# Gate tiles shared between VectorE and GpSimd, and the softmax totals brought to their rows by fewer transfers

## The chip, the cores and the metric

The kernel runs on one core of one Trainium2 chip. The metric is the device time of one execution in microseconds; the time shown for a kernel is the median of its runs. A profile of a single execution lists, per engine, every instruction with its start and its duration: PE (TensorE) multiplies matrices, DVE (VectorE) and POOL (GpSimd) do elementwise arithmetic, ACT (ScalarE) does functions, copies and roundings, and SP (SyncE) only issues DMA transfers, in order, from one queue. Every engine takes its instructions in the order in which they were laid down; an instruction that has to wait holds up all that stand behind it.

## The reference

One layer of a decoder trunk over x of 512 tokens by 2048 channels, all in float32:

```python
mod = silu(c) @ w_ada + b_ada                      # 2048 -> 6144
shift, scale, gate = split(mod, 3)
h = rms_norm(x, norm_g) * (1 + scale) + shift
z = h @ w_in                                       # columns: u_a v_a g_a q_b k_b v_b g_b f_b
y_a = u_a' * (tril(w_s) @ LayerNorm(v_a') + b_s) * silu(g_a)     # 8 groups, chunks of 128 tokens
y_b = softmax(q k^T / 8 + F[t] - F[s], causal) @ v * silu(g_b)   # 16 heads of 64, F = cumsum(log sigmoid f)
out = rms_norm(x + gate * (concat(y_a, y_b) @ w_out), final_g)
```

Two pieces matter here. The vector **gate**, the last third of `mod`, is a product of a vector of 2048 with a matrix of 2048 by 2048 and is needed only when the output projection is done. The **softmax** is normalised ahead: the logarithm of each row's total is subtracted inside the exponent, so the totals have to get into an operand of the score matmul.

## The kernel before, in words

**Products.** Every float32 operand of a large matmul is taken apart into a rounded upper part (hi) and the remainder (lo), and each product is three matmuls: hi by hi, hi by lo, lo by hi (L147 to L149 with the weights as the stationary operand, L156 to L158 with the tokens). `w_tile` loads one weight tile of 512 KB into a buffer named `raw` (L125), ScalarE rounds it to `whi` (L131), VectorE subtracts to get `wlo` (L132). There are four `raw` buffers and two each of `whi` and `wlo`. A weight tile of the second half feeds 24 matmuls of 128x512.

**Order.** The instruction order of each engine is not the order of the text. A planner with a timeline model of its own lays the instructions out; `tc.high_priority(offset=150)` in `w_tile` lets a weight tile's load and split be drawn ahead of other work, and `tc.issue_after(ins)` pins an instruction behind `ins` in the queue of the engine that both use. After each weight tile, `tick()` runs one entry of `slots` (attention or mixer steps) and one entry of `fillers` (side work).

**The gate.** 32 of the fillers are `gate_step(g, i)`, for g of 0 to 3 (512 columns each) and i of 0 to 7. Each loads a gate tile, two blocks of 128x512 (L601), into the same four `raw` buffers that the weight tiles use; GpSimd multiplies each block by its column of silu(c) (L606, L608) and adds it to `gate[:, g, :]` (L609). `gate_sum(g)` then adds over the partitions with a matmul by ones (L668) and adds the bias (L669). After the gates, `sum_part` fills the ticks with sums of output weights on GpSimd (L654).

**The softmax totals.** For each of four groups u of four heads, `score_head` computes the row maxima `nm` and the totals `rs` (both 128 partitions by 16: four heads by four blocks of tokens), and `lse()` takes the logarithm (L502), subtracts (L503), transposes the 128x16 block on TensorE (L505), takes the result apart into hi and lo (`lt`, L66 on ScalarE and L67 on VectorE) and writes each head's hi row and lo row into two rows of the second query operand `QS[i][1]`, with one DMA from SP for each row: 8 transfers of 2 KB (L512). `probs(i)` multiplies that operand in L529. `lt` in the trace is the source of these transfers and `q` their destination.

**Around it.** In the order of the trace: norm and conditioning, the first big column groups (st), value products of group A (va), then the attention part (q, k, gb, vb groups, four times), and the output projection (wo). The lines at issue lie in the attention part.

Of the kernel before, what the change touches and what calls it, by code (L numbers as in the profile page):

```python
# [8 lines left out]
F32 = mybir.dt.float32  # L9
F32R = mybir.dt.float32r  # L10
BF16 = mybir.dt.bfloat16
AF = mybir.ActivationFunctionType
ALU = mybir.AluOpType
AX = mybir.AxisListType

P = 128
# [11 lines left out]
def trunk_kernel(  # L28
# [17 lines left out]
    nc = tc.nc  # L46
# [12 lines left out]
    def bank(tag, name):  # L59
        if tag == "x":  # L60
            tag = "bbbc"[turn[0] % 4]
            turn[0] += 1
        return ps.tile([P, 512], F32, tag=tag, name=name, bufs={"mm": 4, "b": 3, "c": 1}[tag])

    def split(hi, lo, src, eng=None):
        a = nc.scalar.activation(hi, src, AF.Copy)  # L66
        return a, (eng or nc.vector).tensor_tensor(lo, src, hi.bitcast(F32), ALU.subtract)  # L67


    ident = const.tile([P, P], F32, name="ident")  # L70
# [45 lines left out]
    WPRI = 150  # L116
    EPRI = 150

    def w_tile(segs, k0, nk, src=win_r, name="", pri=WPRI, loeng=None):
        n = sum(w for _, w in segs)  # L120
        with tc.high_priority(offset=pri):
            raw = wp.tile([P, nk, n], F32, tag="raw", name=f"raw_{name}", bufs=4)
            o = 0
            for c0, w in segs:
                newest_w[0] = (load if pri == 0 else nc.sync.dma_start)(  # L125
                    raw[:, :, o : o + w], src[:, k0 : k0 + nk, c0 : c0 + w]
                )
                o += w
            hi = wp.tile([P, nk, n], F32R, tag="whi", name=f"whi_{name}")
            lo = wp.tile([P, nk, n], F32R, tag="wlo", name=f"wlo_{name}")  # L130
            nc.scalar.activation(hi, raw, AF.Copy)  # L131
            (loeng or nc.vector).tensor_tensor(lo, raw, hi.bitcast(F32), ALU.subtract)  # L132
        return hi, lo
# [72 lines left out]
    sc = const.tile([P, KB], F32, name="sc")  # L206
# [10 lines left out]
    gate = gp_.tile([P, 4, 512], F32, name="gate")  # L217
# [135 lines left out]
    def new_y(b):  # L353
        y[b] = act.tile([P, S], F32, tag="ya" if b < 8 else "yb", bufs=8, name=f"y{b}")
# [7 lines left out]
    for q, (k0, nk) in enumerate(CH):  # L362
# [10 lines left out]
        for si, sid in enumerate(order):  # L373
# [9 lines left out]
            for kk in range(k0, k0 + nk, st_k):  # L383
                for gi, (segs, bl) in enumerate(grp):
                    hi, lo = w_tile(
                        segs, kk, st_k, name=f"st{q}_{sid}_{gi}_{kk}", pri=0,
# [29 lines left out]
    pb = ctx.enter_context(tc.tile_pool(name="pb", bufs=1))  # L416
    QS, KS = [], []
# [18 lines left out]
    def halves(e):  # L436
        return (slice(0, 64), slice(64, 128)) if e == 0 else (slice(64, 128), slice(0, 64))
# [35 lines left out]
    def attention_slots(u):  # L473
        nms, rss, lts = {}, {}, {}
        ptt = {}

        def score_head(i):
            if i == 0:
                nms[0] = pb.tile([P, 16], F32, name=f"nm{u}", tag="nm", bufs=1)
                rss[0] = pb.tile([P, 16], F32, name=f"rs{u}", tag="rs", bufs=1)  # L480
            nm, rs = nms[0], rss[0]
            q1, q2 = QS[i]
            k1, k2 = KS[i]
            for t in range(NT):
                n = (t + 1) * P
                tsl = slice(t * P, n)
                cx = slice(4 * i + t, 4 * i + t + 1)
                s_ = bank("x", f"s{u}_{i}_{t}")
                nc.tensor.matmul(s_[:, 0:n], q1[:, tsl], k1[:, 0:n], start=True, stop=False)
                nc.tensor.matmul(s_[:, 0:n], q2[:, tsl], k2[:, 0:n], start=False, stop=True)  # L490
                nc.vector.tensor_tensor_reduce(
                    out=s_[:, 0:n], in0=s_[:, 0:n], in1=cmask[:, S - n : S], scale=1.0,
                    scalar=3.0e38, op0=ALU.add, op1=ALU.min, accum_out=nm[:, cx],
                )
                nc.scalar.activation(
                    s_[:, 0:n], s_[:, 0:n], AF.Exp, bias=nm[:, cx], scale=-1.0,
                    accum_out=rs[:, cx],
                )

        def lse():  # L500
            nm, rs = nms[0], rss[0]
            nc.scalar.activation(rs, rs, AF.Ln)  # L502
            nc.vector.tensor_tensor(nm, nm, rs, ALU.subtract)  # L503
            lp = bank("x", f"lse{u}")
            nc.tensor.transpose(lp[0:16, 0:P], nm, ident)  # L505
            lt = pb.tile([16, 2, P], F32R, name=f"lt{u}", tag="lt", bufs=1)
            split(lt[:, 0, :], lt[:, 1, :], lp[0:16, 0:P])
            for i in range(4):
                _, o = halves(i % 2)
                s2 = QS[i][1]  # L510
                for r_ in range(2):
                    nc.sync.dma_start(  # L512
                        s2[o.start + r_ : o.start + r_ + 1, :].bitcast(F32),
                        lt[4 * i : 4 * i + 4, r_, :].bitcast(F32),
                    )

        def probs(i):
            h = 4 * u + i
            q1, q2 = QS[i]
            k1, k2 = KS[i]  # L520
            pth = pb.tile([P, 1280], F32R, name=f"pth{h}", tag="pth")
            ptl = pb.tile([P, 1280], F32R, name=f"ptl{h}", tag="ptl")
            ptt[i] = (pth, ptl)
            for j in range(NT):
                n = S - j * P
                ssl = slice(j * P, (j + 1) * P)
                t_ = bank("x", f"t{h}_{j}")
                nc.tensor.matmul(t_[:, 0:n], k1[:, ssl], q1[:, j * P : S], start=True, stop=False)
                nc.tensor.matmul(t_[:, 0:n], k2[:, ssl], q2[:, j * P : S], start=False, stop=True)  # L529
                nc.vector.tensor_tensor(t_[:, 0:P], t_[:, 0:P], cmaskT, ALU.add)  # L530
                pr = pb.tile([P, S], F32, name=f"p{h}_{j}", tag="p", bufs=2)
                nc.scalar.activation(pr[:, 0:n], t_[:, 0:n], AF.Exp, scale=-1.0)
                osl = slice(OFF[j], OFF[j] + n)
                split(pth[:, osl], ptl[:, osl], pr[:, 0:n])

        def values(i):
            h = 4 * u + i
            b = 2 * u + i // 2
            e = i % 2
            pth, ptl = ptt[i]  # L540
            op = bank("x", f"o{h}")
            for buf in (pth, ptl):
                for j in range(NT):
                    nc.tensor.matmul(
                        op[:, j * P : S], vs_[0][:, j, i, :], buf[:, OFF[j] : OFF[j] + S - j * P],
                        start=(buf is pth and j == 0), stop=(buf is ptl and j == NT - 1),
                    )
            a, o = halves(e)
            if e == 0:
                new_y(8 + b)  # L550
            tm = pb.tile([P, S], F32, name=f"tm{h}", tag="th", bufs=2)
            nc.scalar.activation(tm[a], op[o], AF.Copy, scale=0.5)
            late = b not in sgb
            nc.vector.scalar_tensor_tensor(
                y[8 + b][a] if late else tm[a], op[a], 0.5, tm[a], ALU.mult, ALU.add
            )
            if not late:
                nc.vector.tensor_tensor(y[8 + b][a], tm[a], sgb[b][a], ALU.mult)

        c_ = lambda f, *a: (lambda: f(*a))  # L560
        return [
            [c_(score_head, 0), c_(score_head, 1)],
            [c_(score_head, 2), c_(score_head, 3)],
            [c_(lse)],
            [c_(probs, 0)],
            [c_(values, 0), c_(probs, 1)],
            [c_(values, 1), c_(probs, 2)],
            [c_(values, 2), c_(probs, 3)],
            [c_(values, 3)],
        ]  # L570
# [28 lines left out]
    def gate_step(g, i):  # L599
        ga = wp.tile([P, 2, 512], F32, tag="raw", name=f"gate{g}_{i}", bufs=4)  # L600
        nc.sync.dma_start(ga, ada_r[:, 2 * i : 2 * i + 2, 2, g * 512 : (g + 1) * 512])  # L601
        for j in range(2):
            kk = 2 * i + j
            a = gate[:, g, :]
            if kk == 0:
                nc.gpsimd.tensor_scalar(a, ga[:, j], sc[:, 0:1], None, ALU.mult)  # L606
            else:
                nc.gpsimd.tensor_scalar(ga[:, j], ga[:, j], sc[:, kk : kk + 1], None, ALU.mult)  # L608
                nc.gpsimd.tensor_tensor(a, a, ga[:, j], ALU.add)  # L609


    dram = ctx.enter_context(tc.tile_pool(name="dram", bufs=1, space=bass.MemoryType.DRAM))
# [203 lines left out]
    for g in range(4):  # L816
        for i in range(8):
            gates.append(lambda g=g, i=i: gate_step(g, i))
            if g and i == 2:
                gates.append(lambda g=g: gate_sum(g - 1))  # L820
# [73 lines left out]
    r = [[None] * 4 for _ in range(NT)]  # L894
# [259 lines left out]
```

## Time and profile before

| what | value |
|---|---|
| median of 3 runs | 905.56 us (905.46 to 912.02) |
| the profiled execution: its time | 903.07 us |
| the profiled execution: its span, first to last instruction | 901.3 us |
| mean granted TensorE clock | 0.988 |
| busy: PE, DVE, ACT, POOL | 878.5, 596.3, 444.6, 438.1 us |

The span is what the rows of the trace add up to; the time of the execution holds 1.8 us around it. Rows of instruction groups give line, engine, operation, output<-inputs by the program's names, shapes, count | busy us, mean ns of one | idle us of the engine just before them and what ended it. Rows of a timeline give start, duration, engine, line and operation. Rows of waits give engine, line and the releaser: total us, times, longest us.

### The profile page before, as it was taken

The numbers are of one execution on the slowest core, as the hardware profiler recorded it, in microseconds if no ns is written. First come the engines' busy times: TensorE is split into PE (matmuls) and PEld (weight loads), VectorE is DVE, ScalarE is ACT, GpSimd is POOL, SyncE is SP. The second block draws the span as 40 slices with busy tenths as digits, with TensorE's granted clock in tenths as the row PEclk, the third lists the DMA queues.
The fourth block names the chain that finished last, engine by engine and source line by source line (L and its number), as shares of the span: only waits on it lengthen the run. The fifth ranks groups of instructions, "written<-read, shape, count | busy, mean of one in ns | idle before, by whom it ended". The sixth has DMA issues, their size and how long they took to land.

```text
span 901.3 us, 12686 instructions
## 1 busy us (share of the span) xinstructions
PE 878.5 (97%) x4408; PEld 744.5 (83%) x4408; DVE 596.3 (66%) x982; ACT 444.6 (49%) x775; POOL 438.1 (49%) x338
## 2 busy tenths in 40 slices
PE   6999999999999999999999999999999999999995
PEld 4988888887888997778789888998898888888884
DVE  4768888374436866455786563456764679997687
ACT  5653332442213224465666554557465657554454
POOL 2355555425676359988998879444751000000001
PEclk7899999999999999999999999999999999999998
DMA  9999996438996164554554545677576246577575
GB/s 339 352 352 356 354 318 212 121 108 292 312 317 201 40 186 124 161 161 133 174 165 140 166 130 187 199 234 221 186 249 188 71 126 209 182 252 248 177 238 203
DMA packets 139712, 188.91 MB, mean 210 GB/s; under 512 B 9968, under 2 KB 103360, under 8 KB 139136
## 3 DMA queue, kind: packets, MB, share of 16 engines
q1 hardware_dynamic: 139216, 187.53, 65.0%
q8 instruction: 35, 0.57, 0.3%
q10 hardware_dynamic: 432, 0.57, 0.2%
q14 instruction: 29, 0.24, 0.1%
HBM read 166.90 MB, written 20.97 MB: 208 GB/s over the span
## 4 chain that ended last, share of the span: by engine, by line
PE 88%; DVE 4%; DMA 3%; issue 2%; ACT 2%; POOL 0%; SPq 0%; POOLq 0%; ACTq 0%; DVEq 0%
PE s L149 6%; PE s L147 6%; PE s L148 6%; PE vb L156 3%; PE vb L157 3%; PE vb L158 3%; PE va L158 3%; PE va L156 3%; PE va L157 3%; PE q L147 3%; PE q L149 3%; PE q L148 3%; PE gb L149 3%; PE k L149 3%; PE gb L148 3%; PE gb L147 3%
## 5 line engine op out<-in xcount | busy, mean ns | idle before, releaser
L608 POOL TENSOR_SCALAR gate<-gate,sc 128x512 f32<-128x512 f32 x60 | 106.4, 1783 | 22.6 <-DMA gate<-in_w_ada_dram 13.6
L132 POOL TENSOR_TENSOR wlo_st<-raw_st,whi_st 128x1024 fp32r<-128x1024 f32 (+3 forms) x36 | 68.4, 1905 | 51.3 <-ACT whi_st L131 48.0
L609 POOL TENSOR_TENSOR gate<-gate,gate 128x512 f32<-128x512 f32 x60 | 91.7, 1530 | 1.8
L148 PE MATMUL s<-hl,whi_st 128*128 128x512 f32 x224 | 86.8, 390 | 0.0
L147 PE MATMUL s<-hh,whi_st 128*128 128x512 f32 x224 | 86.7, 392 | 0.0
L654 POOL TENSOR_TENSOR ts<-ts 128x256 f32<-128x256 f32 x64 | 57.1, 898 | 58.2 <-DMA ts<-in_w_out_dram 55.3
L66 ACT ACTIVATE whi_p<-p 128x1024 fp32r<-128x1024 f32 x52 | 55.2, 1061 | 55.1 <-PE woZ L938 20.1
L67 DVE TENSOR_TENSOR wlo_p<-p,whi_p 128x1024 fp32r<-128x1024 f32 x52 | 63.4, 1221 | 20.2 <-ACT whi_p L66 20.1
L246 DVE SCALAR_TENSOR_TENSOR acc<-ada,sc,acc 128x512 f32<-128x512 f32 x98 | 73.9, 754 | 3.4 <-DMA ada<-in_w_ada_dram 0.5
L149 PE MATMUL s<-hh,wlo_st 128*128 128x512 f32 x224 | 76.2, 392 | 0.0
L157 PE MATMUL vb<-whi_vb,hl 128*128 128x256 f32 (+1 forms) x256 | 72.2, 285 | 0.0
L156 PE MATMUL vb<-whi_vb,hh 128*128 128x256 f32 (+1 forms) x256 | 72.0, 285 | 0.0
L158 PE MATMUL vb<-wlo_vb,hh 128*128 128x256 f32 (+1 forms) x256 | 71.3, 288 | 0.0
L981 POOL TENSOR_TENSOR sfin<-sfin,nhalf 128x1 f32<-128x1 f32 x2 | 1.5, 748 | 137.7 <-DVE sfin L1073 137.7
L131 ACT ACTIVATE whi_st<-raw_st 128x1024 fp32r<-128x1024 f32 (+3 forms) x36 | 31.3, 871 | 65.1 <-PE s L148 38.8
L147 PE MATMUL q<-hh,whi_q 128*128 128x512 f32 x128 | 50.6, 395 | 1.3 <-ACT whi_q L131 1.3
L132 DVE TENSOR_TENSOR wlo_va<-raw_va,whi_va 128x1024 fp32r<-128x1024 f32 x16 | 26.0, 1626 | 38.0 <-ACT whi_va L131 33.9
L147 PE MATMUL k<-hh,whi_k 128*128 128x512 f32 x128 | 50.2, 392 | 0.7 <-ACT whi_k L131 0.7
L147 PE MATMUL gb<-hh,whi_gb 128*128 128x512 f32 x128 | 50.4, 394 | 0.3 <-ACT whi_gb L131 0.3
L156 PE MATMUL va<-whi_va,hh 128*128 128x512 f32 x128 | 50.3, 393 | 0.0
L148 PE MATMUL q<-hl,whi_q 128*128 128x512 f32 x128 | 50.2, 392 | 0.0
L148 PE MATMUL gb<-hl,whi_gb 128*128 128x512 f32 x128 | 50.2, 392 | 0.0
(308 smaller groups left out, 2541.9 us busy)
## 6 DMA issues: line engine op xcount, KB each, us to landing
ada<-in_w_ada_dram SPq DMA_DIRECT2D x128, 256.0 KB
gate<-in_w_ada_dram SPq DMA_DIRECT2D x32, 512.0 KB
p<-ts SPq DMA_DIRECT2D x32, 512.0 KB
p<-in_w_out_dram SPq DMA_DIRECT2D x24, 512.0 KB
raw_va<-in_w_in_dram SPq DMA_DIRECT2D x16, 512.0 KB
raw_q<-in_w_in_dram SPq DMA_DIRECT2D x16, 512.0 KB
raw_k<-in_w_in_dram SPq DMA_DIRECT2D x16, 512.0 KB
raw_gb<-in_w_in_dram SPq DMA_DIRECT2D x16, 512.0 KB
```

The source lines that it names most:

```text
L67: return a, (eng or nc.vector).tensor_tensor(lo, src, hi.bitcast(F32), ALU.subtract)
L132: (loeng or nc.vector).tensor_tensor(lo, raw, hi.bitcast(F32), ALU.subtract)
L147: nc.tensor.matmul(pt, hi[:, j, cs], hh[k], start=(k == first), stop=False)
L148: nc.tensor.matmul(pt, hi[:, j, cs], hl[k], start=False, stop=False)
L149: nc.tensor.matmul(pt, lo[:, j, cs], hh[k], start=False, stop=(k == last))
L156: nc.tensor.matmul(o, ah[k][:, tsl], hi[:, j, :], start=(k == first), stop=False)
L157: nc.tensor.matmul(o, al[k][:, tsl], hi[:, j, :], start=False, stop=False)
L158: nc.tensor.matmul(o, ah[k][:, tsl], lo[:, j, :], start=False, stop=(k == last))
L246: nc.vector.scalar_tensor_tensor(sb if kk == KB - 1 else a, ga[:, j], col, a, ALU.mult, ALU.add)
L608: nc.gpsimd.tensor_scalar(ga[:, j], ga[:, j], sc[:, kk : kk + 1], None, ALU.mult)
L609: nc.gpsimd.tensor_tensor(a, a, ga[:, j], ALU.add)
L654: nc.gpsimd.tensor_tensor(dst, l, r, ALU.subtract)
```

## The change

First, in `gate_step`, every second tile (i even) is multiplied and summed on VectorE: one tensor_scalar and one scalar_tensor_tensor make `p`, the weighted sum of the two blocks, in place; GpSimd adds `p` to the accumulator in one instruction. For i = 0, VectorE writes the accumulator itself and GpSimd does nothing. Tiles with i odd are done on GpSimd as before.

Second, in `lse`, the split into hi and lo comes before the transpose: ScalarE rounds the 128x16 block, VectorE subtracts, into one tile `n2` ordered by head, part and token block; one transpose of 128x32 and one ScalarE copy make `lt` of 32 rows, in which a head's hi and lo rows stand together, so one transfer of 8 pieces brings both: four transfers instead of eight.

Third, in `w_tile`, a list `pins`: of the weight tiles that follow an `lse` in the text, the fifth is issued behind that `lse`'s last row transfer.

```diff
+    pins = []
+
     def w_tile(segs, k0, nk, src=win_r, name="", pri=WPRI, loeng=None):
         n = sum(w for _, w in segs)
-        with tc.high_priority(offset=pri):
+        es = ExitStack()
+        for p in list(pins):
+            p[0] -= 1
+            if p[0] < 0:
+                es.enter_context(tc.issue_after(p[1].ins))
+                pins.remove(p)
+        with es, tc.high_priority(offset=pri):
             raw = wp.tile([P, nk, n], F32, tag="raw", name=f"raw_{name}", bufs=4)
...
             lp = bank("x", f"lse{u}")
-            nc.tensor.transpose(lp[0:16, 0:P], nm, ident)
-            lt = pb.tile([16, 2, P], F32R, name=f"lt{u}", tag="lt", bufs=1)
-            split(lt[:, 0, :], lt[:, 1, :], lp[0:16, 0:P])
+            n2 = pb.tile([P, 4, 2, 4], F32R, name=f"n2_{u}", tag="n2", bufs=1)
+            split(n2[:, :, 0, :], n2[:, :, 1, :], nm.rearrange("p (i t) -> p i t", t=4))
+            nc.tensor.transpose(lp[0:32, 0:P], n2.rearrange("p i r t -> p (i r t)").bitcast(F32), ident)
+            lt = pb.tile([32, P], F32R, name=f"lt{u}", tag="lt", bufs=1)
+            nc.scalar.activation(lt, lp[0:32, 0:P], AF.Copy)
             for i in range(4):
                 _, o = halves(i % 2)
-                s2 = QS[i][1]
-                for r_ in range(2):
-                    nc.sync.dma_start(
-                        s2[o.start + r_ : o.start + r_ + 1, :].bitcast(F32),
-                        lt[4 * i : 4 * i + 4, r_, :].bitcast(F32),
-                    )
+                rows_in = nc.sync.dma_start(
+                    QS[i][1][o.start : o.start + 2, :].bitcast(F32),
+                    lt[8 * i : 8 * i + 8, :].bitcast(F32),
+                )
+            pins.append([4, rows_in])
...
         nc.sync.dma_start(ga, ada_r[:, 2 * i : 2 * i + 2, 2, g * 512 : (g + 1) * 512])
+        a = gate[:, g, :]
+        if i % 2 == 0:
+
+            p = ga[:, 0] if i else a
+            nc.vector.tensor_scalar(p, ga[:, 0], sc[:, 2 * i : 2 * i + 1], None, ALU.mult)
+            nc.vector.scalar_tensor_tensor(
+                p, ga[:, 1], sc[:, 2 * i + 1 : 2 * i + 2], p, ALU.mult, ALU.add
+            )
+            if i:
+                nc.gpsimd.tensor_tensor(a, a, p, ALU.add)
+            return
         for j in range(2):
             kk = 2 * i + j
-            a = gate[:, g, :]
-            if kk == 0:
-                nc.gpsimd.tensor_scalar(a, ga[:, j], sc[:, 0:1], None, ALU.mult)
-            else:
-                nc.gpsimd.tensor_scalar(ga[:, j], ga[:, j], sc[:, kk : kk + 1], None, ALU.mult)
-                nc.gpsimd.tensor_tensor(a, a, ga[:, j], ALU.add)
+            nc.gpsimd.tensor_scalar(ga[:, j], ga[:, j], sc[:, kk : kk + 1], None, ALU.mult)
+            nc.gpsimd.tensor_tensor(a, a, ga[:, j], ALU.add)
```

## The prediction, made before the changed kernel ran

> **What bounds the kernel now.** I read the busy table first, then the stretch in which both edits lie (windows), then what TensorE waited for in it.
>
> ```profile
> span 901.3 us, 12686 instructions
> PE 878.5 (97%) x4408; PEld 744.5 (83%) x4408; DVE 596.3 (66%) x982; ACT 444.6 (49%) x775; POOL 438.1 (49%) x338
> ```
>
> ```profile
> 330.00:430.00 100.00, 97.21 (x451) 78.95 (x451) 55.17 (x85) 49.59 (x95) 87.62 (x54) 1.00 0.49 155
> 430.00:564.00 134.00, 133.21 (x718) 115.38 (x719) 84.69 (x150) 76.85 (x158) 119.51 (x79) 1.00 0.51 157
> 564.00:745.00 181.00, 180.11 (x1029) 158.70 (x1028) 111.19 (x221) 107.67 (x226) 65.11 (x75) 1.00 0.60 186
> ```
>
> ```profile
> PE q L147 <- ACT whi_q L131: 1.3, 1, 1.3
> PE t L529 <- DMA q<-lt: 0.9, 1, 0.9
> PE o L544 <- DVE ptl L67: 0.8, 1, 0.8
> PE k L147 <- ACT whi_k L131: 0.7, 1, 0.7
> PE gb L147 <- ACT whi_gb L131: 0.3, 1, 0.3
> PE k L149 <- DVE wlo_k L132: 0.3, 1, 0.3
> ```
>
> TensorE is busy 97% of the span, and the edits take no matmul from it: the transpose is still one instruction, wider by 16 columns. So they can win only TensorE's idle time where gates and totals are made. The windows (length; busy PE, PEld, DVE, ACT, POOL; clock) give it: 100 - 97.21 = 2.79 us, 134 - 133.21 = 0.79, 181 - 180.11 = 0.89, together **4.47 us**; the six longest waits add up to 4.3 of it. The granted clock is 1.00 throughout, so the throttle plays no part. The other idle time, in the first 50 us and in the last 50, is out of reach.
>
> GpSimd is nearly full there (87.62 of 100 and 119.51 of 134). Yet it is not TensorE that waits for it, but SP:
>
> ```profile
> SPq L125 <- POOL gate L609: 51.3, 18, 9.6
> SPq L601 <- POOL gate L609: 23.4, 7, 8.1
> ```
>
> ```profile
> 345.52 0.37 SPq L125 DMA_DIRECT2D raw_k<-in_w_in_dram  x1
> 354.10 0.37 SPq L601 DMA_DIRECT2D gate<-in_w_ada_dram  x1
> 354.56 0.42 SPq L125 DMA_DIRECT2D raw_k<-in_w_in_dram  x1
> ```
>
> ```profile
> 393.32 1.68 DVE L132 TENSOR_TENSOR wlo_gb<-raw_gb,whi_gb 128x1024 fp32r<-128x1024 f32 x1 [2.16 <-ACT whi_gb L131]
> 395.05 0.50 PE L149 MATMUL gb<-hh,wlo_gb 128*128 128x512 f32 x1
> ```
>
> ```profile
> 545.67 1.23 DVE L132 TENSOR_TENSOR wlo_k<-raw_k,whi_k 128x1024 fp32r<-128x1024 f32 x1 [4.42 <-ACT whi_k L131]
> 551.25 0.39 PE L149 MATMUL k<-hh,wlo_k 128*128 128x512 f32 x1
> ```
>
> A gate tile sits in a `raw` buffer until GpSimd is through, and SP's queue stood 51.3 + 23.4 = 74.7 us behind such buffers. At 345.52 to 354.10 a gate load holds up the weight load behind it. What reaches TensorE depends on the lead of the weights. At 393 us the remainder tile is ready at 393.32 + 1.68 = 395.00 and used at 395.05: no lead. At 545 us it is ready at 546.90 and used at 551.25: 4.35 us. So in 330 to 430 weights come just in time, and 2.79 of the 4.47 us are lost there; later the lead hides most of GpSimd's lateness.
>
> **The change part by part.** The gate arithmetic:
>
> ```profile
> L608 POOL TENSOR_SCALAR gate<-gate,sc 128x512 f32<-128x512 f32 x60 | 106.4, 1783 | 22.6 <-DMA gate<-in_w_ada_dram 13.6 <-issue 6.4 <-DVE vs L67 2.4
> L609 POOL TENSOR_TENSOR gate<-gate,gate 128x512 f32<-128x512 f32 x60 | 91.7, 1530 | 1.8
> L606 POOL TENSOR_SCALAR gate<-gate,sc 128x512 f32<-128x512 f32 x4 | 8.3, 2076 | 2.2 <-DMA gate<-in_w_ada_dram 2.1
> L768 DVE TENSOR_SCALAR va<-va,mv,rsv 128x512 f32<-128x512 f32 x8 | 4.7, 616 | 0.4 <-POOL rsv L91 0.4
> L986 DVE TENSOR_SCALAR c<-c,sfin 128x512 f32<-128x512 f32 x4 | 1.8, 480 | 0.0
> L246 DVE SCALAR_TENSOR_TENSOR accs<-ada,sc,accs 128x512 f32<-128x512 f32 x10 | 7.5, 751 | 0.7 <-DMA ada<-in_w_ada_dram 0.5
> ```
>
> *Off GpSimd:* 16 of the 32 tiles lose both multiplications (4 of L606, 28 of L608) and, per g, four of 15 additions (one for i = 0; one each for i = 2, 4, 6): 4 x 2.076 + 28 x 1.783 + 16 x 1.530 = 82.7 us of 206.4. All of it lies beside TensorE and is worth nothing itself; it is worth the earlier buffers.
>
> *On VectorE:* 16 tensor_scalar, between 0.480 and 0.616 us, and 16 scalar_tensor_tensor at 0.751: 19.7 to 21.9 us, 1.37 us a pair at most. VectorE is busy 55.17 + 84.69 of 234 us there and would come to about 160. The cover is the weights' lead: with 4.35 us a pair costs nothing; with 0.05 us it costs TensorE what it delays, unless the weights come sooner.
>
> *A wait moves with it.* The first VectorE instruction of a pair waits for the gate tile's transfer; behind it stand `wlo`, the softmax rows and the evacuations, and TensorE waits for those. GpSimd's waits of this kind show the size (13.6 us in 12 of 32 tiles; half the tiles would give about 7 us):
>
> ```profile
> POOL gate L608 <- DMA gate<-in_w_ada_dram: 13.6, 12, 2.9
> ```
>
> *The totals:*
>
> ```profile
> 418.34 6.34 SPq L512 DMA_DIRECT2D q<-lt  x8
> 424.80 0.37 SPq L125 DMA_DIRECT2D raw_q<-in_w_in_dram  x1
> ...
> 495.98 5.09 SPq L512 DMA_DIRECT2D q<-lt  x8
> 604.01 5.22 SPq L512 DMA_DIRECT2D q<-lt  x8
> 686.73 5.26 SPq L512 DMA_DIRECT2D q<-lt  x8
> ```
>
> ```profile
> 424.80 3.93 DMA raw_q<-in_w_in_dram
> 428.75 1.06 ACT whi_q L131
> 429.86 0.50 PE q L147
> ```
>
> ```profile
> L502 ACT ACTIVATE rs<-rs 128x16 f32<-128x16 f32 x4 | 0.9, 216 | 0.0
> ```
>
> Eight issues hold SP for 5.09 us at least, 0.64 each; four at that price 2.5 us. The transfer of eight pieces instead of four isn't in the trace; I bound it by 0.37 (the weight load's row) and twice 0.64, and take 0.64, the nearest kind. SP gets back 21.9 - 10.2 = 11.7 us. The chain of waits shows where that counts: the weight load at 424.80 stood behind the eight rows, landed 3.93 us later, and TensorE began its tile at 429.86 after the 1.3 us wait of the list above. Four rows end some 3 us earlier: that 1.3 us goes. The 0.9 us (L529 waiting for the rows of the last group) goes too: its rows left SP from 686.73 on, head 0 needs one transfer instead of two, and the pin keeps a weight load of that time behind the rows. Against it: the chain gains a hop, a ScalarE rounding before the transpose (0.22 us by L502's row, 1.06 more, as at 428.75, if a `whi` split stands in front). I cost this at nothing, covered by the halved queue; uncovered, 0.2 to 1.3 us in each of four groups.
>
> *What is left of the waits.* 0.7 and 0.3 (the k group at 363 us, behind the late load at 354.56): I count 0.7 won. 0.8 (`ptl`): half. The 0.3 of gb: 0.2. Sum of gains: 1.3 + 0.9 + 0.7 + 0.4 + 0.2 = **3.5 us**, bounds 0 and 4.5. What is added: GpSimd's 87.62 us in 330 to 430 are some 14 gate tiles (206.4 / 32 = 6.45 us each), so seven become pairs; most meet a longer lead than now because SP is freed; I charge **1.0 us**, bounds 0 and the second rival's 9. Net -2.5: an execution of 903.07 would become 900.6. It lies 2.5 us under the median of the runs, 905.56, and I forecast against the latter: **903.0 us**.
>
> The two elementwise engines slow each other here:
>
> ```profile
> 445.77 4.25 DVE L132 TENSOR_TENSOR wlo_k<-raw_k,whi_k 128x1024 fp32r<-128x1024 f32 x1 [1.03 <-ACT whi_k L131]
> 445.75 2.53 POOL L609 TENSOR_TENSOR gate<-gate,gate 128x512 f32<-128x512 f32 x2
> 448.26 1.56 POOL L608 TENSOR_SCALAR gate<-gate,sc 128x512 f32<-128x512 f32 x1
> ```
>
> This subtraction takes 1.23 us at 545.67 and 4.25 us beside three gate instructions of GpSimd: 3.0 us lost in one instruction. [...] In the sum I let it cancel: 82.7 us less GpSimd also block `wlo` less.
>
> **The rivals.**
>
> *All of the waits go.* GpSimd's gate work is then 40% lighter, the ring of `raw` buffers never holds SP, and the pairs are hidden: -4.5 us, 901.0. For it: the 74.7 us of SP; against it: the 0.8 us has another cause.
>
> *VectorE takes the place of GpSimd: slower.* Place: 330 to 430 us. It decides from the point where what stands ahead of a `wlo` exceeds the weights' lead there (0.05 us at 393). Price: a pair of 1.37 us, plus a mean wait for its tile of 13.6 / 12 = 1.1, less about 1 us of lead, 1.5 us on each of seven tiles, is 10; less the waits won, +7 to +10 us: 913 to 916. A single block of 3.0 us per pair would give more. For it: VectorE waits in order, GpSimd's lateness hurt only through the ring. Against it: VectorE is idle 45% of that stretch.
>
> *The change doesn't do what it says.* The ring is released no earlier, because an even tile now waits for VectorE's queue and then for GpSimd's, and the rows leave no earlier, because the extra hop eats the shorter queue. Then all the waits stay, if in another place: 905.5, within 1.5.
>
> **How the numbers follow.** Forecast 0.50; all waits gone or a little better 0.12; no change 0.22; VectorE 0.16, of which half stays under 1% because the lead has grown. One per cent is 9 us, about what a measurement of this kernel can tell from no change. Faster by over 1% would need twice the idle time found, by another layout of the planner: 0.04 of the second case. So faster 0.04, slower 0.08, within 0.88. Range: below, 901.0 less the 2.5 us by which executions of one kernel differ, 898.5; above, into the VectorE case, 909.5.
>
> **What would show it.** Right: gate instructions of GpSimd at about 124 us, four row transfers of 2 to 3 us per group, SP's wait for L609 well under 74.7 us, TensorE's idle time in these stretches near 2 us. Wrong: VectorE idle ahead of the pairs on gate transfers over 7 us, `wlo` ready later than TensorE wants it in 330 to 430, TensorE waiting on L529 for the rows in more than one group, or a changed tail after 850 us.

## The result: slower by 0.6%, and where the profile after shows it

The changed kernel takes 911.26 us (median of 22 runs, 909.13 to 917.14), the kernel before 904.88 us beside it; the ratio is 1.0062, with an interval of 1.0046 to 1.0079. The forecast was 903.0, in a range of 898.5 to 909.5, so sign and range were both missed. Executions of one kernel differ by the clock granted in the first 50 us of the span (0.69 in some of the profiled ones, 0.83 to 0.90 in the others), so what is compared below are the measured ratios with their intervals, which are not the quotients of the medians.

The busy table and the three stretches of the changed kernel, columns as before:

```profile
span 908.1 us, 12618 instructions
PE 881.1 (97%) x4408; PEld 745.5 (82%) x4408; DVE 614.2 (68%) x1014; ACT 445.3 (49%) x779; POOL 357.4 (39%) x290
...
330.00:430.00 100.00, 96.26 (x446) 78.30 (x445) 60.68 (x96) 48.64 (x94) 52.14 (x34) 1.00 0.53 161
430.00:564.00 134.00, 130.64 (x693) 111.39 (x692) 92.55 (x167) 76.02 (x159) 71.91 (x51) 0.99 0.49 150
564.00:745.00 181.00, 179.63 (x1028) 158.52 (x1027) 108.47 (x212) 105.14 (x222) 66.37 (x74) 1.00 0.57 180
```

GpSimd is 80.7 us lighter (82.7 were worked out). TensorE's idle time went up: 3.74 us in the first stretch (2.79 before), 3.36 in the second (0.79), 1.37 in the third (0.89), together 8.47 where it was 4.47. Its longest waits in 320 to 745:

```profile
PE t L537 <- ACT p L541: 1.9, 1, 1.9
PE k L157 <- DVE wlo_k L140: 1.7, 1, 1.7
PE o L553 <- DVE ptl L67: 1.5, 1, 1.5
PE t L538 <- DMA q<-lt: 1.4, 1, 1.4
PE gb L157 <- DVE wlo_gb L140: 1.1, 1, 1.1
```

Three of these five name VectorE's products (`wlo`, `ptl`); the first names ScalarE, which itself was waiting for VectorE, as the timeline further down shows. (Lines moved: `wlo` is L140, the pair L615 and L616, GpSimd's additions L620 and L625, the row transfers L520.) What VectorE waited for in 320 to 570, and what GpSimd waited for there:

```profile
DVE gate L615 <- DMA gate<-in_w_ada_dram: 38.9, 13, 4.9
```

```profile
POOL gate L624 <- DMA gate<-in_w_ada_dram: 31.1, 10, 5.2
POOL gate L620 <- DMA gate<-in_w_ada_dram: 5.4, 1, 5.4
```

In 13 of its 16 pairs VectorE stood still for the gate tile's transfer, 3.0 us each and up to 4.9. How one of them reaches TensorE is a few lines of the timeline (from three engines, put in order of time):

```profile
448.75 1.55 DVE L615 TENSOR_SCALAR gate<-gate,sc 128x512 f32<-128x512 f32 x1 [2.09 <-DMA gate<-in_w_ada_dram]
450.22 0.29 DVE L539 TENSOR_TENSOR t<-t,cmaskT 128x128 f32<-128x128 f32 x1
450.60 0.49 ACT L541 ACTIVATE p<-t 128x384 f32<-128x384 f32 x1 [3.49 <-DVE t L539]
451.14 0.33 PE L537 MATMUL t<-q,k 128*128 128x128 f32 x1 [1.87 <-ACT p L541]
```

VectorE waits 2.09 us for the tile, then needs 1.55 for a multiplication that takes 0.48 alone; behind it stands a softmax mask, ScalarE waits 3.49 us for that, and TensorE 1.87 us for ScalarE's exponent to free a bank. The stall has a second price, right behind it:

```profile
452.50:456.00 3.50, 3.50 (x11) 2.79 (x10) 3.47 (x5) 1.74 (x5) 2.45 (x2) 0.52 0.70 211
```

In these 3.5 us the mean granted clock is 0.52, and the seven matmuls of 512 columns in them start 0.43 us apart instead of 0.23: 1.4 us more. With the 4.0 us of idle time that makes 5.4 of the 6.8 us by which the two profiled spans differ (901.3 and 908.1).

### The profile page after: what moved, and what is told of

It is laid out like the page before. It is cut to its first block, busy times and chain, and to the rows that moved or that the text cites. A ratio compares the mean times of both kernels' runs of the same rounds, so it can differ in the third digit from the quotient of the medians.

```text
span 908.1 us, 12618 instructions
## 1 busy us (share of the span) xinstructions
PE 881.1 (97%) x4408; PEld 745.5 (82%) x4408; DVE 614.2 (68%) x1014; ACT 445.3 (49%) x779; POOL 357.4 (39%) x290
## 4 chain that ended last, share of the span: by engine, by line
PE 77%; DMA 8%; DVE 8%; issue 2%; POOL 2%; ACT 2%; SPq 1%; POOLq 0%; DVEq 0%; ACTq 0%
PE s L155 6%; PE s L157 6%; PE s L156 6%; DMA gate<-in_w_ada_dram 3%; PE va L166 3%; PE va L164 3%; PE va L165 3%; PE vb L164 3%; PE vb L165 3%; PE vb L166 3%; PE k L156 2%; PE k L157 2%; PE k L155 2%; PE q L156 2%; PE q L155 2%
## 5 line engine op out<-in xcount | busy, mean ns | idle before, releaser
L140 POOL TENSOR_TENSOR wlo_st<-raw_st,whi_st 128x1024 fp32r<-128x1024 f32 (+3 forms) x36 | 68.4, 1904 | 51.4 <-ACT whi_st L139 49.1
L624 POOL TENSOR_SCALAR gate<-gate,sc 128x512 f32<-128x512 f32 x32 | 57.0, 1791 | 58.9 <-DMA gate<-in_w_ada_dram 31.1
L254 DVE SCALAR_TENSOR_TENSOR acc<-ada,sc,acc 128x512 f32<-128x512 f32 x98 | 73.9, 754 | 5.0 <-DMA ada<-in_w_ada_dram 2.1
L140 DVE TENSOR_TENSOR wlo_va<-raw_va,whi_va 128x1024 fp32r<-128x1024 f32 x16 | 24.9, 1557 | 39.6 <-ACT whi_va L139 39.6
L157 PE MATMUL gb<-hh,wlo_gb 128*128 128x512 f32 x128 | 50.3, 394 | 1.1 <-DVE wlo_gb L140 1.1
L157 PE MATMUL k<-hh,wlo_k 128*128 128x512 f32 x128 | 49.5, 397 | 1.7 <-DVE wlo_k L140 1.7
L156 PE MATMUL k<-hl,whi_k 128*128 128x512 f32 x128 | 50.6, 395 | 0.0
```

The lines of the kernel that those rows point to most:

```text
L156: nc.tensor.matmul(pt, hi[:, j, cs], hl[k], start=False, stop=False)
L157: nc.tensor.matmul(pt, lo[:, j, cs], hh[k], start=False, stop=(k == last))
L254: nc.vector.scalar_tensor_tensor(sb if kk == KB - 1 else a, ga[:, j], col, a, ALU.mult, ALU.add)
```

## The experiments

The theories: **1**, VectorE's in-order wait for the gate tile costs; **2**, the rows do the harm (SP waited 17.0 us for `lt`, 1.2 + 0.7 us for its two halves before); **3**, the pair's arithmetic, or its blocking beside GpSimd, costs. The planner's layout differs between kernels, so beside the ratios I compare TensorE's idle time in 330 to 564 us: 3.58 us before, 7.09 after. The same window holds slightly different work in each kernel.

**One edit at a time.** The gate edit alone (`gate_step` as changed, `lse` and `w_tile` as before):

> The kernel before with the gate edit alone (eight row transfers, no pins). Theory 1, VectorE stands in its queue until the gate tile's transfer has landed and TensorE pays for it: most of the loss is here, 4 to 7 us over the kernel before, and VectorE waits over 25 us for gate tiles. Theory 2, the rows do the harm (SP stood 17.0 us waiting for lt): within 1.5 us of the kernel before.

Measured: 908.23 us, ratio 1.0042 (1.0012 to 1.0073), TensorE idle 8.35 us. That is 3.8 us, between 1.1 and 6.6, so theory 1 is favoured by the time, but not by much. VectorE waited 30.7 us for gate tiles, as theory 1 has it:

```profile
DVE gate L606 <- DMA gate<-in_w_ada_dram: 30.7, 12, 4.8
```

The row edit with its pins alone (`lse` and `w_tile` as changed, `gate_step` as before):

> The kernel before with the row edit and the pins alone. Theory 1: between 2 us faster and 1 us slower than the kernel before. Theory 2: 4 to 6 us slower, with SP waiting over 10 us for lt.

Measured: ratio 0.9996 (0.9963 to 1.0030), idle 3.53 us. Theory 2 falls: the rows alone cost nothing that can be seen, and win nothing that can be seen either.

**The same arithmetic without the wait.**

```diff
+            r0, r1 = (hh[2 * i + z].bitcast(F32) for z in range(2))
-            p = ga[:, 0] if i else a
+            p = gsc[0] if i else a          # a tile of its own
-            nc.vector.tensor_scalar(p, ga[:, 0], ...)      # and ga[:, 1]
+            nc.vector.tensor_scalar(p, r0, ...)            # and r1
-                nc.gpsimd.tensor_tensor(a, a, p, ALU.add)
+                nc.gpsimd.tensor_tensor(a, a, ga[:, 0], ALU.add)
```

> The changed kernel, but the two VectorE instructions of a pair read resident blocks of the activations instead of the gate tile and (for i over 0) write a tile of their own; GpSimd adds the tile's first block. So VectorE does the same arithmetic and waits for no gate tile; half of the gate's products are left out. Theory 1: 4 to 7 us come back, the time is within 2 us of the kernel before. Theory 3, the arithmetic itself or its blocking beside GpSimd is what costs: the time stays within 2 us of the changed kernel, 6 us over before.

Measured: 919.89 us, ratio 1.0169 (1.0122 to 1.0216). Neither theory had that, and it has a reason of its own: with nothing to wait for, the planner laid the pairs out far ahead.

```profile
L620 DVE TENSOR_SCALAR gsc<-hh,sc x12: 473/483/1756, 119.9 to 195.4; 128x512 f32<-128x512 f32 x12
L620 DVE TENSOR_SCALAR gate<-hh,sc x4: 481/481/481, 38.1 to 39.3; 128x512 f32<-128x512 f32 x4
```

They ran between 38 and 196 us, in the big column groups, and TensorE lost 11.5 of the 150 us from 50 to 200. This run cannot judge the theories; it shows that pairs in that early stage delay TensorE: its longest wait there, 4.0 us, is for a sum that VectorE makes among the pairs (`accs`, L254).

**The wait without the arithmetic.**

```diff
+            n = 8 if i else 512
-            nc.vector.tensor_scalar(p, ga[:, 0], ...)      # 512 columns
+            nc.vector.tensor_scalar(p[:, 0:n], ga[:, 0, 0:n], ...)   # second instruction alike
```

> The changed kernel, but for i over 0 the two VectorE instructions work on 8 columns of the gate tile instead of 512: the wait for the tile stays and nearly all the arithmetic goes (12 of 16 pairs; the gate's other columns miss one product). Theory 1: within 2 us of the changed kernel, 4 to 7 us over before. Theory 3: within 2 us of the kernel before.

Measured: ratio 1.0083 (1.0049 to 1.0118), idle 7.83 us. With 12 of 16 pairs down to 8 columns nothing came back. That speaks against theory 3, but less than the edit suggests: the instructions of 8 columns still take 0.469 and 0.652 us on average, and all pairs together 20.8 us of VectorE's time, where the changed kernel has 26.8. The next run is the stronger one.

```profile
DVE gate L616 <- DMA gate<-in_w_ada_dram: 32.9, 12, 5.8
```

**The arithmetic in place, without the wait.** The third run again, with the pair pinned behind VectorE's newest weight split:

```diff
+            with tc.issue_after(newest_wlo[0].ins):
                 nc.vector.tensor_scalar(p, r0, ...)
                 nc.vector.scalar_tensor_tensor(p, r1, ...)
```

> As the run before it with resident data, but each pair is issued behind the newest remainder subtraction (wlo) on VectorE, so that it stays in the stretch from 330 to 564 us and is not laid out early. Half of the gate's products are left out. Theory 1 (the wait for the gate tile costs): within 2 us of the kernel before, and TensorE idle under 3 us in 330 to 564. Theory 3 (the arithmetic and its blocking cost): 4 us or more over the kernel before.

Measured: 903.32 us, ratio 0.9970 (0.9946 to 0.9994), idle 1.75 us. No wait for gate tiles is left among VectorE's, while the pairs still take 26.5 us of its time. So theory 3 falls as the main cause: the same arithmetic in the same stretch, without the wait, leaves the kernel no slower than the one before.

**A repair: the whole computation, each pair one weight tile later.**

```diff
+    due = []
     def gate_step(g, i):
+        while i % 2 and due:
+            due.pop(0)()
         if i % 2 == 0:
-            (pair and GpSimd's addition)
+            def pair():
+                with tc.issue_after(newest_wlo[0].ins):
+                    (pair)
+                (GpSimd's addition)
+            due.append(pair)
```

> The changed kernel with each pair held back by one weight tile: it is issued behind the wlo subtraction of the next weight tile, so that its gate tile has mostly landed when VectorE comes to it. All of the computation is there. Theory 1: VectorE waits under 10 us for gate tiles and the time is within 3 us of the kernel before, on either side. Theory 3: 4 us or more over the kernel before. Theory 4 (both edits are harmless alone and the row chain is what VectorE's waits stretch): SP's wait for lt falls under 5 us with VectorE's waits.

Measured: 900.67 us, ratio 0.9975 (0.9948 to 1.0003), idle 1.42 us. The pair's first instruction, and what GpSimd still waited for:

```profile
L625 DVE TENSOR_SCALAR gate<-gate,sc 128x512 f32<-128x512 f32 x16 | 12.3, 772 | 0.0
```

```profile
POOL gate L636 <- DMA gate<-in_w_ada_dram: 43.5, 12, 7.4
```

This pair of rows shows the difference best. The idle time ahead of L625 is 0.0 us (39.0 in the changed kernel), while GpSimd waits 43.5 us for gate tiles, more than the 36.5 of the changed kernel, and TensorE is not the worse for it: apart from a few fills and sums, gate work alone stands behind it in its queue, while softmax and splits stand behind VectorE's. The gain over the kernel before is not clear of noise in this run. Theory 4, that the rows suffer from VectorE's waits, falls too: SP still waited 14.6 us for `lt` here.

```profile
SPq L523 <- ACT lt L520: 14.6, 3, 5.5
```

The same without the row edit:

> The same with the gate edit alone: eight row transfers, no pins. Theory 1: as the run with both edits, within 2 us. If the row edit does harm of its own beside the gate edit, this one is faster than the run with both by 2 us or more.

Measured: 901.5 us, ratio 0.9958 (0.9923 to 0.9993), the same as with both edits within what can be told.

**What the freed GpSimd is worth.**

```diff
         if i % 2 == 0:
-            (pair on VectorE; GpSimd adds p)
+            (GpSimd adds ga[:, 0]; copies it for i = 0)
```

> The changed kernel without the VectorE pairs: of every second gate tile GpSimd adds (for i = 0 copies) the first block, with one instruction; half of the products are left out. It is what the freed GpSimd is worth when VectorE pays nothing. The prediction's gain without its loss: 1 to 5 us faster than the kernel before, 900 to 904. If GpSimd's lateness never mattered: within 1 us of it.

Measured: 899.36 us, ratio 0.9943 (0.9915 to 0.9971), idle 0.79 us. The gain that the prediction counted is there; this kernel has the row edit too.

**The wait alone, on the kernel before.**

```diff
+        if i % 2 == 0:
+            nc.vector.tensor_scalar(ft[:, 0, 0:8], ga[:, 0, 0:8], sc[:, 0:1], None, ALU.mult)
```

> The kernel before, all arithmetic of the gate on GpSimd as there, and one VectorE instruction on 8 columns of every second gate tile added, whose result is not used (GpSimd's product of that block stands behind it, since it overwrites what is read). So only the wait comes to VectorE's queue. Theory 1: VectorE waits over 20 us for gate tiles and the time is 4 to 14 us over the kernel before. Theory 3 (arithmetic or blocking): within 2 us of it.

Measured: ratio 1.0073 (1.0039 to 1.0106), idle 7.85 us: as theory 1 says for the time, but not for the waits, which are 10.5 us where over 20 were expected and the changed kernel has 38.9:

```profile
DVE ft L603 <- DMA gate<-in_w_ada_dram: 10.5, 8, 3.8
```

So 10.5 us of waiting went with as much harm as 38.9. The 16 tiny instructions are in a chain with GpSimd here (its first product waits for them), one of them waited 2.8 us for matmuls that still read `ft`, into which they write, and GpSimd is still full. So more than a wait was added; which share is whose I did not separate, and the sum of VectorE's waits does not by itself give the loss.

**Is it the lag or the pin?** The pair pinned behind the split of its own tick:

> The changed kernel with each pair issued behind the wlo of the weight tile of its own tick, not of the next one. It tells whether the pin alone or the lag of one tile takes the wait away. Theory 1: if VectorE still waits over 10 us for gate tiles, 2 us or more over the kernel with the lag; if the pin alone ends the waits, equal to it, 899 to 903.

Measured: 901.1 us, ratio 0.9950 (0.9921 to 0.9979), idle 0.92 us; VectorE's wait for gate tiles is 0.2 us. The pin is enough: the changed kernel's fault was where the planner put the pair, not its work.

```profile
DVE gate L619 <- DMA gate<-in_w_ada_dram: 0.2, 1, 0.2
```

The three versions with late or pinned pairs stand at 0.9950 to 0.9975 of the kernel before; two of their intervals lie under 1, and all lie under that of the changed kernel.

## Why the prediction was wrong, by its own steps

**The bound and the gain: right within the noise.** TensorE's idle time near the gates was the prize, put at 3.5 us and at most 4.5. With GpSimd relieved and no pairs on VectorE, 0.0057 of 905 is 5.2 us, between 2.6 and 7.7; the idle time of the three stretches fell from 4.47 to 1.54 us. Whether it came by earlier buffers, as predicted, is open: weights do get ahead (in 330 to 430 a remainder of q, k or gb is ready 1.4 us before its first use on average in the kernel before and 3.0 in the relief kernel), but VectorE's own work gets shorter as well (590.5 us busy, against 596.3 before and 600.2 with the row edit alone).

**GpSimd's relief and VectorE's arithmetic: right for GpSimd, a fifth low for VectorE.** Predicted about 124 us of gate work on GpSimd and 19.7 to 21.9 us on VectorE:

```profile
L616 DVE SCALAR_TENSOR_TENSOR gate<-gate,sc 128x512 f32<-128x512 f32 x12 | 12.5, 1044 | 0.1
L615 DVE TENSOR_SCALAR gate<-gate,sc 128x512 f32<-128x512 f32 x16 | 11.3, 703 | 39.0 <-DMA gate<-in_w_ada_dram 38.9
L616 DVE SCALAR_TENSOR_TENSOR gate<-gate,sc,gate 128x512 f32<-128x512 f32 x4 | 3.0, 744 | 0.0
```

GpSimd's three groups come to 122.2 us (57.0 + 45.5 + 19.7); VectorE's to 26.8. Much of the excess is in the scalar_tensor_tensor of the twelve (1.044 us), and the trace tells why: eight of them took 0.73 to 0.75 us, and four 1.55 to 1.78, each of which began while GpSimd was adding two blocks. One of each kind, and GpSimd's two additions beside the first (the second began at 515.70):

```profile
514.16 2.89 POOL L625 TENSOR_TENSOR gate<-gate,gate 128x512 f32<-128x512 f32 x2
515.82 1.78 DVE L616 SCALAR_TENSOR_TENSOR gate<-gate,sc 128x512 f32<-128x512 f32 x1
541.42 0.75 DVE L616 SCALAR_TENSOR_TENSOR gate<-gate,sc 128x512 f32<-128x512 f32 x1
```

The eight that took 0.73 to 0.75 us began while GpSimd was not adding. In the kernel before, the subtraction of 4.25 us at 445.77 began beside two such additions, and the one of 1.23 us at 545.67 ran within two multiplications of GpSimd (544.17 to 548.33). GpSimd took longer there too: a first multiplication (L606) took 3.59 us at 440.17, with VectorE's subtraction of 441.19 beside it, where the four of that line have a median of 1.57 us. The prediction let this slowing cancel in its sum; no run shows that term by itself. What the runs showed in its place is that VectorE as a whole is only 17.9 us busier (596.3 to 614.2), less than the 26.8 us that its pairs take, so as a sum it did cancel. The cost of the arithmetic in place is the step from the relief kernel to the pinned one without waits, 0.9943 to 0.9970: some 2.4 us, with intervals that overlap. That is above the 1.0 us charged; by itself it would have left the change faster.

**The step that failed: "a wait moves with it".** It was seen and named, and sized at 7 us, 1.1 us in each case, from GpSimd's own waits in the kernel before (13.6 us in 12 of 32 tiles). VectorE's waits came to 38.9 us, 3.0 on average in 13 cases, far over the 7 us that the prediction gave as a sign of being wrong. The row was taken from an engine that came late to its tiles: a full GpSimd found most of them landed. Taken off the late engine, the tiles are met before they have landed, and the consumers of the changed kernel waited 38.9 + 31.1 + 5.4 = 75.4 us for them. The size of the wait went with where the consumer was laid out: the same pairs behind a weight split waited 0.2 us.

**The cover that failed with it: "most meet a longer lead than now because SP is freed".** For that reason the sum charged 1.0 us for the pairs, waits and all. SP was hardly freed; it stood 66.8 us behind GpSimd's gate buffers, where it stood 74.7:

```profile
SPq L133 <- POOL gate L625: 31.3, 6, 6.0
SPq L610 <- POOL gate L625: 15.7, 6, 5.2
SPq L133 <- POOL gate L620: 11.9, 7, 4.4
SPq L610 <- POOL gate L620: 7.9, 3, 3.5
```

The mean lead of the remainders of q, k and gb (from ready to first use, at eight matmuls a tile) went from 1.4 to 2.0 us in 330 to 430, with five of 16 under 0.5 us in both kernels, and from 4.5 down to 3.4 in 430 to 564.

**The second rival was the case that came.** VectorE took GpSimd's place as forecast there, +7 to +10 us, against 5.6 by the ratio; it was given 0.16. That its size came near is in part luck: it counted 1.1 us of wait on seven tiles, and 3.0 us on 13 came. Its place was in part wrong: the first stretch (330 to 430), where weights had no lead, lost 0.95 us of TensorE time, the second, which the lead of 4.35 us was to cover, 2.57. TensorE's two long waits in the second are for the softmax chain (1.9 us for the exponent, 1.5 for `ptl`), those in the first for `wlo` (1.7 and 1.1). So the lead did cover `wlo`, but not the softmax chain, which also stands behind the pair and has no such lead. That cover was claimed for too much. And one per cent was taken for about what a measurement can tell from no change; the interval here is 0.16% either way.

**The missing term.** Behind one stall TensorE's clock came down for 3.4 us, 1.4 us of the loss; the prediction had put the throttle at no part.

**The rows: the queue time right, the gain not seen.** Four transfers hold SP for 2.6 to 2.9 us, as the estimate of 0.64 each had it:

```profile
419.53 2.73 SPq L520 DMA_DIRECT2D q<-lt  x4
422.36 0.37 SPq L133 DMA_DIRECT2D raw_q<-in_w_in_dram  x1
```

I counted 1.3 + 0.9 us won. With the row edit alone the 1.3 us wait for `whi_q` is indeed gone, and the 0.9 became 0.5, but the wait for `ptl` rose from 0.8 to 1.8, so idle time fell by 0.05 us in 330 to 564 and by 0.36 in the third stretch (0.89 to 0.53). The extra hop, costed at nothing, let SP wait 8.5 us for `lt` there instead of 1.9, at no price that can be seen.

By ratios, with different layouts and intervals of 1.5 to 3 us either way, so roughly: relief -5.2 us, arithmetic in place +2.4, the waits and what follows from them +8.3 (from 0.9970 to 1.0062), together +5.6.

## What to carry to other kernels

Before work is moved to an engine, ask what stands behind it in that engine's queue: here 43.5 us of waiting for transfers were harmless on the side engine, and 38.9 us were dear on the engine that feeds TensorE. Don't size that wait from the old engine if the old engine was late. The time from issue to landing, 3.93 us for a weight load in the kernel before, would have been the nearer size: the 13 waits were 3.0 us on average and 4.9 at most. If the move is worth having, pin the consumer behind an instruction whose own input was loaded at about the same time: here that turned 0.6% slower into 0.25 to 0.5% faster, the lower of which is not clear of noise.

## What the runs showed of the hardware that I had not expected

TensorE's clock came down after pauses much shorter than I would have looked for. In the changed kernel, an idle time of 1.87 us at 449 us was followed within 1.5 us by 3.4 us at half the clock. The kernel with pairs of 8 columns shows it again, after 1.99 us idle from 352. Single idle times of 1.75 us (changed kernel, 363), 1.8 (pairs of 8 columns, ahead of a `k` tile) and four of 1.5 to 1.7 us (gate edit alone) had no such trace. At the end of the changed kernel TensorE had stood idle for 5.25 us when the clock fell at 903.17, and at the end of the kernel before for 4.88 us when it fell at 896.73. So no one length of a pause fits what was measured.

What the traces of the changed kernel and the kernel before do show is a grid. In the former the clock falls at 8.88, 29.36, 452.61 and 903.17 us, which lie 6, 124 and 132 times 3.413 us apart, and in the latter at 9.26, 26.33 and 896.73, 5 and 255 times 3.413 us apart; the low clock that began at 452.61 lasted 3.41 us. Sorted by steps of this length, the steps ahead of two of the falls, and the steps behind them, are these, first in the changed kernel, then in the one with pairs of 8 columns (length; busy PE, PEld, DVE, ACT, POOL; clock, DMA):

```profile
449.20:452.61 3.41, 1.54 (x8) 1.27 (x8) 3.31 (x4) 2.01 (x4) 2.65 (x3) 1.00 0.04 8
452.61:456.02 3.41, 3.41 (x10) 2.73 (x9) 3.38 (x5) 1.65 (x4) 2.34 (x2) 0.50 0.71 214
351.86:355.27 3.41, 1.42 (x7) 1.06 (x7) 3.41 (x3) 0.10 (x1) 3.21 (x1) 1.00 0.20 71
355.27:358.68 3.41, 3.41 (x10) 2.67 (x9) 3.21 (x5) 1.03 (x2) 0.00 (x0) 0.50 0.69 217
```

TensorE was idle for 1.87 and 1.99 us of the two steps ahead of the falls. The idle time of 1.75 us at 363 fell into two steps, 0.41 us into the first and 1.34 into the second, and the clock stayed at 1.00. In 330 to 745 of the kernel before and of the changed one, the largest idle time of a step that no fall followed is 1.48 us (changed kernel, 517.46). So in this stretch it turned somewhere between 1.48 and 1.87 us, about half a step; that isn't sharp, since near the end of the changed kernel, at 896.34, a step with 1.83 us idle was not followed by a fall.
